# First three weight tiles side by side, and the operands of the first Strassen job, its silus and the last transposes made at other places, in a one-core encoder layer

## The chip, the cores and the metric

The kernel runs on one core of one Trainium2 chip. The metric is device time in microseconds (us) of one execution, lower is better. A profiled execution also leaves a trace: the rows of every engine (PE is the matrix engine, DVE, ACT and POOL the vector, scalar and GpSimd engines, SP the engine that issues most transfers) with start, length, and what ended the idle time before them.

## The reference

One layer of a streaming encoder on x of 512 tokens x 1024 channels, float32. Only what the change touches is shown.

```python
f = swiglu(rms_norm(h, ffn1_pre_g), w1, w3, w2)      # (silu(x @ w1) * (x @ w3)) @ w2, D_FF = 2816
h = h + 0.5 * rms_norm(f, ffn1_post_g)
u = rms_norm(h, mix_pre_g)
q, k, v, xr, xg = jnp.split(u @ w_in, splits, axis=-1)
...                                                  # recurrent branch, attention with a relative bias, gates
h = h + rms_norm(merged @ w_o, mix_post_g)
f = swiglu(rms_norm(h, ffn2_pre_g), v1, v3, v2)
h = h + 0.5 * rms_norm(f, ffn2_post_g)
```

## The kernel before

**Precision by splitting.** Every float32 operand of a product is split in two parts that PE takes at full rate: `hi` is a rounded copy made by ACT, `lo` the rest, made by DVE (`split2`, L182 to L185; `split_to`, L142 to L152 for weights). A product is three matmuls, hi x hi, lo x hi and hi x lo (L194 to L196 for 512 or 256 token columns in `mm_feat`; L212 to L214 in `mm_tok`; L440 to L442 in `mm_s`, 256 columns). `uT` holds the current activation, transposed and split, for all channels.

**Units.** A unit is one 128-row tile of a weight matrix against all tokens: 8 slices of 128 channels x 3 matmuls. The weights come in the order of the list `order`. `get` keeps a few units ahead: `dma_to` issues a tile's load (512 KB, on SP), `split_to` splits it.

**Slots.** Nearly all tiles in on-chip memory are taken from one pool of 42 slots of 4 KB per partition; a new tile takes the slot that has been free longest, and its first writer, a transfer or an engine, waits until the last reader of the tile before it is done. The transfers on SP also share eight completion semaphores in turn, so a ninth waits for the first. Products go to 8 PSUM banks.

**Order by hand.** The order of instructions on each engine is the order of the program. `later(n, fn)` puts a piece of work n points ahead; `point()` is called twice in each unit and once in each Strassen product and emits what is due. `point(True)` emits all that is left.

**The start** (L558 to L612). Nine matmuls on zeros warm PE up. The constants `vec`, the first weight tile in two parts and the eight slices of x (transposed) are loaded on SP, then three more weight tiles and the token-major copy `h`. Slice by slice, ACT and DVE scale x with the first norm's gain and split it into uT (L594, L595). Then three units run one after another on them, without the norm's factor 1/rms. That factor is computed from `h` meanwhile (squares L600, `rstd_of`), turned into `dgs`, a diagonal matrix per 128 tokens, and broadcast over partitions by PE (L609) into `Rb`; `silu_mul` (L393 to L404) applies it afterwards. Behind L609 stands a small product for the table of relative biases (L641). DVE copies it (L643), and one transfer issued by POOL writes it, repeated for 128 rows, to `bias_scr` in device memory (L646). Attention reads that much later.

**Units, then Strassen.** Tiles 2 to 5 of w1 and w3 of the first FFN run as units (`swiglu_units`). Meanwhile `norm_x` makes x normalised in plain float32 (`xn`), `sums` (L660) four sums of its quarters, and some of these quarters are split into slots of their own (`to_slots`). The rest of w1 and w3 is computed by `Pairs`: two weight tiles and the tokens in two halves, in 2 x 2 blocks, make one job with seven products in place of eight (Strassen's scheme in Winograd's form). A job needs its operands, made by `prep(m, i)`: i = 0 makes four sums of blocks of the weights (S12 and S34, on POOL, L482 to L485), i = 1, 2, 3 split the first tile, S12 and S34, i = 4 the block a22. `run` (L498 to L554) goes through the jobs, w1 and w3 in turn, and prepares job n + 1 between the products of job n. ACT copies out the partial results q1 (L513), q5 (L515), u (L520) and v (L532). Two banks, `bu` and `bx`, collect several products, so the next product into one waits for the copy of the last. The seventh product, a22 x t4, comes after two products of the next job (`last`). For w1's jobs the result c goes through a silu on ACT: two thirds of it at the job's end (L535, L536), the rest in `last` (L548). For job 0 four operands are written into uT (`to_uT`, L703 to L706), which only works after the last unit has read it.

The second FFN does the same (NC2 = 4 units' tiles there), with most of its operands from uT itself.

**The down projections and the wo product** (`tok_gemm`, L305). Four token tiles are finished one after another; each is normed (`norms`), transposed by PE (L285) and split into uT (L294, L295); for the second FFN a plain float32 copy `xf` is kept as well (L302). For the last tile PE meanwhile runs the first half of the tokens (columns 0 to 255) of the next four units (L374 to L381), then the last transposes (L382), then the second halves.

Of the kernel before, what the change touches and what calls it, by code (L numbers as in the profile page):

```python
# [10 lines left out]
F32 = mybir.dt.float32  # L11
# [4 lines left out]
P = 128  # L16
# [35 lines left out]
def hybrid_layer(ctx: ExitStack, tc: tile.TileContext, a: dict, out: bass.AP):  # L52
# [80 lines left out]

    def dma_to(n):
        while st["dma"] < min(n, len(order)):
            nm, i = order[st["dma"]]
            r = slot([P, D], name=f"raw_{nm}{i}")
            sp.dma_start(out=r, in_=a[nm][i * P : (i + 1) * P, :])
            raws[st["dma"]] = r
            st["dma"] += 1  # L140
# [76 lines left out]
    def rstd_of(ssq, scale=1.0, during=lambda: None):  # L217
# [9 lines left out]
        during()  # L227
# [17 lines left out]
    def post_norm(acc, t, gpost, scale, dst, after=None):  # L245
# [8 lines left out]
        r = rstd_of(ss, scale, lambda: dve.tensor_tensor(out=fg[:, cs[1]], in0=acc[1], in1=gpost[:, cs[1]], op=ALU.mult))  # L254
# [50 lines left out]
    def tok_gemm(nm, xs, n, R, gpost_name, scale, gpre_name, first, x_to=None, xf=None, spill=False):  # L305
# [139 lines left out]
    class Pairs:  # L445
# [3 lines left out]
        def __init__(self, na, nb, f0, X, hid):  # L449
# [3 lines left out]
            self.w, self.c1 = {}, {}  # L453
# [5 lines left out]
        def prep(self, m, i):  # L459
            if m >= len(self.jobs):  # L460
                return
            k = self.k0 + 2 * m
            if i == 0:
                self.raws(m)
# [16 lines left out]
            if i == 0:  # L481
                pool.tensor_tensor(out=s12[:, :QH], in0=a21, in1=a22, op=ALU.add)  # L482
                pool.tensor_tensor(out=s12[:, QH:], in0=s12[:, :QH], in1=a11, op=ALU.subtract)
                pool.tensor_tensor(out=s34[:, QH:], in0=a12, in1=s12[:, QH:], op=ALU.subtract)
                pool.tensor_tensor(out=s34[:, :QH], in0=a11, in1=a21, op=ALU.subtract)  # L485
# [12 lines left out]
        def run(self, tail):  # L498
# [4 lines left out]
            for n, (nm, f) in enumerate(self.jobs):  # L503
# [7 lines left out]
                bu, bx, bc = (bank("c")[:, :256] for _ in range(3))  # L511
                mm_s(W["a11"], X["b11"], bu)
                act.activation(q1, bu, AF.Copy)  # L513
# [20 lines left out]
                if first:  # L534
                    act.activation(c[:, 0, :], c[:, 0, :], AF.Silu)  # L535
                    act.activation(c[:, 1, 256:], c[:, 1, 256:], AF.Silu)  # L536
                else:
# [20 lines left out]
    raw = slot([P, D], name="raw_first")  # L558
    hi, lo = slot([P, D], F32R, name="whi"), slot([P, D], F32R, name="wlo")
    pairs[0] = (hi, lo)  # L560
    st["dma"] = st["split"] = 1
    parts = (slice(0, 2 * P), slice(2 * P, D))
    xts = [slot([P, 2, SEQ], name="xt") for _ in range(KT // 2)]

    def load_x(k):
        sp.dma_start(out=xts[k // 2][:, k % 2, :], in_=a["xT"][k * P : (k + 1) * P, :])
# [580 lines left out]
```

## Time and profile before

| | us |
|---|---|
| three runs | 1150.8, 1151.95, 1152.6 |
| median | 1151.95 |
| profiled execution | 1152.42 |
| its span, first to last instruction | 1150.6 |
| PE busy in it | 1133.9 |
| DVE, ACT, POOL busy | 781.1, 571.7, 355.3 |

The profile lists for each engine rows of the form: start, length (both us), engine, line, operation, output<-inputs, shapes, and in brackets how long the engine was idle before it and which instruction ended that. Matmuls overlap, so their lengths are longer than the distance between their starts; the pace of PE is read from the starts. "xN" at the end of a row means N equal instructions merged. A line such as L185 can be that of a helper: which tile it works on stands in the names.

### The profile page before, as it was taken

Reading aid. Unit: us, or ns where it says so; the run is one execution under the profiler, and the core shown is the slowest. Engines: PE = TensorE matmul, PEld = TensorE weight load, DVE = VectorE, ACT = ScalarE, POOL = GpSimd, SP = SyncE. Lnnn points to the kernel's source line nnn. Section 1 sums busy time; section 2 is a strip of 40 time slices with the busy share of each in tenths; the row PEclk is TensorE's granted clock in tenths of the full one; section 3 lists DMA queues with packets and bytes.
Section 4 is the critical chain, followed back from the end, with each engine's and each line's share of the span. In section 5 each row is a group of like instructions: output and inputs, shape, how many; then the busy total and the mean of one; then the engine's idle time right before and its main releaser. Section 6 shows DMA issues by size and latency. Waiting matters only on the chain.

```text
span 1150.6 us, 17044 instructions
## 1 busy us (share of the span) xinstructions
PE 1133.9 (99%) x6691; PEld 1008.4 (88%) x6691; DVE 781.1 (68%) x1168; ACT 571.7 (50%) x1011; POOL 355.3 (31%) x263
## 2 busy tenths in 40 slices
PE   8989999999999999999999999999999999999997
PEld 6879999988888888888888888889899999998886
DVE  4897788876427755595678864667868688885313
ACT  6345555564324457754656653355545555564211
POOL 0247777600001000001456550000655667700000
PEclk9999999999999999999999999999999999999999
DMA  9663332264312411234132223442033322255101
GB/s 361 108 131 100 111 111 92 76 218 157 105 68 94 164 55 56 73 110 144 41 92 92 79 89 126 149 144 92 19 111 111 106 88 101 93 183 170 50 19 55
DMA packets 35648, 124.93 MB, mean 109 GB/s; under 512 B 4272, under 2 KB 4400, under 8 KB 35568
## 3 DMA queue, kind: packets, MB, share of 16 engines
q1 hardware_dynamic: 33120, 115.41, 30.0%
q0 software_dynamic: 2448, 8.43, 3.9%
q8 instruction: 52, 0.85, 0.3%
q14 instruction: 28, 0.23, 0.1%
HBM read 116.50 MB, written 7.33 MB: 108 GB/s over the span
## 4 chain that ended last, share of the span: by engine, by line
PE 92%; DMA 3%; DVE 2%; ACT 1%; issue 1%; SPq 0%; DVEq 0%; ACTq 0%
PE f L196 11%; PE f L195 11%; PE f L194 11%; PE c L440 10%; PE c L442 10%; PE c L441 10%; PE acc L212 8%; PE acc L214 8%; PE acc L213 8%; DMA bias_scr<-erow 3%; PE pt L962 1%; PE s L926 1%; PE s L925 1%; PE o L978 1%; DMA raw_w3a<-in_w3a_dram 1%; PE o L979 1%
## 5 line engine op out<-in xcount | busy, mean ns | idle before, releaser
L194 PE MATMUL f<-uT,whi 128*128 128x512 f32 (+1 forms) x560 | 206.2, 368 | 2.2 <-ACT uT L594 1.7
L196 PE MATMUL f<-uT,whi 128*128 128x512 f32 (+1 forms) x560 | 205.2, 366 | 0.6 <-DVE uT L295 0.4
L195 PE MATMUL f<-uT,wlo 128*128 128x512 f32 (+1 forms) x560 | 204.8, 366 | 0.8 <-DVE wlo L150 0.8
L212 PE MATMUL acc<-whi,hT 128*128 128x512 f32 x352 | 137.3, 390 | 0.0
L213 PE MATMUL acc<-wlo,hT 128*128 128x512 f32 x352 | 137.1, 390 | 0.0
L214 PE MATMUL acc<-whi,hT 128*128 128x512 f32 x352 | 137.1, 389 | 0.0
L194 PEld LDWEIGHTS f<-uT,whi 128*128 128x128 f32 x560 | 105.7, 189 | 20.8 <-ACT uT L594 2.4
L196 PEld LDWEIGHTS f<-uT,whi 128*128 128x128 f32 x560 | 105.7, 189 | 19.1 <-DVE uT L595 1.3
L195 PEld LDWEIGHTS f<-uT,wlo 128*128 128x128 f32 x560 | 105.7, 189 | 17.6 <-DVE wlo L150 1.1
L185 DVE TENSOR_TENSOR wlo<-S,whi 128x1024 fp32r<-128x1024 f32 x68 | 115.0, 1691 | 8.8 <-ACT whi L184 6.9
L440 PE MATMUL c<-Xh,whi 128*128 128x256 f32 x408 | 116.3, 285 | 4.0 <-ACT ct L513 4.0
L441 PE MATMUL c<-Xh,wlo 128*128 128x256 f32 x408 | 116.2, 285 | 0.0
L442 PE MATMUL c<-Xl,whi 128*128 128x256 f32 x408 | 116.2, 285 | 0.0
L440 PE MATMUL c<-uT,whi 128*128 128x256 f32 x408 | 115.9, 284 | 0.0
L441 PE MATMUL c<-uT,wlo 128*128 128x256 f32 x408 | 115.8, 284 | 0.0
L442 PE MATMUL c<-uT,whi 128*128 128x256 f32 x408 | 115.8, 284 | 0.0
L440 PEld LDWEIGHTS c<-Xh,whi 128*128 128x128 f32 x408 | 78.8, 193 | 4.4 <-ACT ct L513 4.4
L946 POOL TENSOR_SCALAR P<-P,d 128x256 f32<-128x256 f32 (+1 forms) x64 | 63.0, 999 | 55.3 <-DVE d L944 33.6
L442 PEld LDWEIGHTS c<-Xl,whi 128*128 128x128 f32 x408 | 79.0, 194 | 0.0
L441 PEld LDWEIGHTS c<-Xh,wlo 128*128 128x128 f32 x408 | 78.9, 193 | 0.0
L440 PEld LDWEIGHTS c<-uT,whi 128*128 128x128 f32 x408 | 78.7, 193 | 0.0
L441 PEld LDWEIGHTS c<-uT,wlo 128*128 128x128 f32 x408 | 78.7, 193 | 0.0
(300 smaller groups left out, 2641.3 us busy)
## 6 DMA issues: line engine op xcount, KB each, us to landing
raw_w3a<-in_w3a_dram SPq DMA_DIRECT2D x22, 512.0 KB, 4.5
raw_w2a<-in_w2a_dram SPq DMA_DIRECT2D x22, 512.0 KB, 4.2
raw_w1b<-in_w1b_dram SPq DMA_DIRECT2D x22, 512.0 KB, 4.3
raw_w3b<-in_w3b_dram SPq DMA_DIRECT2D x22, 512.0 KB, 4.2
raw_w2b<-in_w2b_dram SPq DMA_DIRECT2D x22, 512.0 KB, 4.3
raw_w1a<-in_w1a_dram SPq DMA_DIRECT2D x21, 512.0 KB, 4.1
raw_wg<-in_wg_dram SPq DMA_DIRECT2D x16, 512.0 KB, 4.0
raw_xr<-in_xr_dram SPq DMA_DIRECT2D x8, 512.0 KB, 4.6
```

What stands on the lines that cost most here:

```text
L185: dve.tensor_tensor(out=lo, in0=src, in1=f32(hi), op=ALU.subtract)
L194: pe.matmul(ps[:, c0:c1], wh[:, s], h_, start=k == 0, stop=False)
L195: pe.matmul(ps[:, c0:c1], wl[:, s], h_, start=False, stop=False)
L196: pe.matmul(ps[:, c0:c1], wh[:, s], l_, start=False, stop=k == KT - 1)
L212: pe.matmul(acc[n], x[:, 0, c], wh[:, s], start=first, stop=False)
L213: pe.matmul(acc[n], x[:, 0, c], wl[:, s], start=False, stop=False)
L214: pe.matmul(acc[n], x[:, 1, c], wh[:, s], start=False, stop=last)
L440: pe.matmul(ps, wh[:, s], xh, start=first, stop=False, skip_group_check=True)
L441: pe.matmul(ps, wl[:, s], xh, start=False, stop=False, skip_group_check=True)
L442: pe.matmul(ps, wh[:, s], xl, start=False, stop=k == 3, skip_group_check=True)
L925: pe.matmul(o, lq, KS[g][:, 0, k0 : k0 + n], start=True, stop=False)
L946: pool.tensor_scalar(out=pt[:, x, b0:256], in0=pt[:, x, b0:256], scalar1=d[:, x : x + 1], scalar2=None, op0=ALU.mult)
```

## The change

- **Start.** Three weight tiles (w1 tile 0, w3 tile 0, w1 tile 1) are loaded in quarters between the slices of x, split in quarters, and for each slice of x PE runs nine matmuls, three for each tile. The first slice of x is issued by ACT, after a tiny square root there, which loads ACT's table. A tiny silu behind the square root of the norm loads the silu table early.
- **Bias table.** Its small product stands ahead of the broadcast of r, the copy is done by ACT, and the store is issued from there on.
- **Job 0 of the first FFN.** Its two weight tiles are loaded out of turn behind `h`. Its sums are made by DVE (behind `dgs`), its splits follow around the first `silu_mul`. Job 1's sums, first and second split are made before the jobs begin, at the places where job 0's stood before.
- **uT for job 0.** One of the four operands is written before job 0; the other three are emitted inside it, behind the copies of q1, q5 and u (`hooks`).
- **Silus.** All three of a w1 job are emitted in `last`, behind a22's product of the next job.
- **Last job of each FFN.** The a12 product stands behind s4 and s3 in place of ahead of them.
- **Last transposes.** They stand ahead of the fourth half unit, with the `xf` copies of the last two tiles behind them.

```diff
+    def dma_one(k):                      # loads order[k] out of turn
+        ...
     def dma_to(n):
         while st["dma"] < min(n, len(order)):
-            ...
+            dma_one(st["dma"])
             st["dma"] += 1
@@ rstd_of
         act.activation(q, v, AF.Sqrt)
-        during()
+        during(q)
@@ tok_gemm
         for i, key in enumerate(first):
             ws.append(get(*key, ahead=len(first) - 1 - i, rawahead=2))
             bs.append(bank("f"))
+            if i == len(first) - 1:
+                trs[t] = transpose_mm(us[t])
+                transpose_out(trs[t], t)
+                if xf:
+                    transpose_xf(trs[t - 1], t - 1, xf)
+                    transpose_xf(trs[t], t, xf)
             mm_feat(bs[i], ws[i], 0, 256)
             if i == 0:
-                tr = transpose_mm(us[t - 1])
+                trs[t - 1] = transpose_mm(us[t - 1])
                 us[t] = norms(acc[t], t, gpost, scale, gpre, spill)
-                transpose_out(tr, t - 1, xf)
-        transpose_out(transpose_mm(us[t]), t, xf)
+                transpose_out(trs[t - 1], t - 1)
@@ Pairs.prep
-        def prep(self, m, i):
-            if m >= len(self.jobs):
+        def prep(self, m, i, eng=None):
+            if m >= len(self.jobs) or (m, i) in self.ready:
                 return
...
-                pool.tensor_tensor(out=s12[:, :QH], in0=a21, in1=a22, op=ALU.add)
+                e = eng or pool
+                e.tensor_tensor(out=s12[:, :QH], in0=a21, in1=a22, op=ALU.add)
...
@@ Pairs.run
+                at = lambda i: [f() for f in hooks.get((n, i), ())]
                 mm_s(W["a11"], X["b11"], bu)
                 act.activation(q1, bu, AF.Copy)
+                at(1)
                 mm_s(W["s1"], X["t1"], bx)
                 act.activation(q5, bx, AF.Copy)
+                at(2)
                 last()
                 ...
                 act.activation(u, bu, AF.Copy)
+                at(3)
...
-                mm_s(W["a12"], X["b21"], bc)
-                del W["a11"], W["a12"]
-                dve.tensor_tensor(out=c[:, 0, :256], in0=bc, in1=q1, op=ALU.add)
+                def c11():
+                    mm_s(W["a12"], X["b21"], bc)
+                    del W["a11"], W["a12"]
+                    dve.tensor_tensor(out=c[:, 0, :256], in0=bc, in1=q1, op=ALU.add)
+                if n < len(self.jobs) - 1:
+                    c11()
...
                 dve.tensor_tensor(out=c[:, 1, 256:], in0=v, in1=q5, op=ALU.add)
-                if first:
-                    act.activation(c[:, 0, :], c[:, 0, :], AF.Silu)
-                    act.activation(c[:, 1, 256:], c[:, 1, 256:], AF.Silu)
-                else:
+                if n == len(self.jobs) - 1:
+                    c11()
+                if not first:
...
                     if first:
                         act.activation(c[:, 1, :256], bu, AF.Silu)
+                        act.activation(c[:, 0, :], c[:, 0, :], AF.Silu)
+                        act.activation(c[:, 1, 256:], c[:, 1, 256:], AF.Silu)
@@ start
+    tiny = small(4, "tiny")
+    dve.memset(tiny, 1.0)
+    act.activation(tiny, tiny, AF.Sqrt)
+    load_x(0, act)
     sp.dma_start(out=vec, in_=a["vec"])
-    sp.dma_start(out=raw[:, parts[0]], in_=a["w1a"][0:P, parts[0]])
-    load_x(0)
-    load_x(1)
-    sp.dma_start(out=raw[:, parts[1]], in_=a["w1a"][0:P, parts[1]])
-    for k in range(2, KT):
-        load_x(k)
-    dma_to(4)
+    for kp in range(KT // 2):
+        load_w(0, kp)
+        if kp:
+            load_x(2 * kp)
+        load_w(1, kp)
+        load_w(2, kp)
+        load_x(2 * kp + 1)
+    dma_to(NS + 2)
     h_load([a["x"][t * P : (t + 1) * P, :] for t in range(NT)])
+    pairs_a = Pairs("w1a", "w3a", NC1, X1, hid)
+    dma_one(pairs_a.k0)
+    dma_one(pairs_a.k0 + 1)
...
     for k in range(KT):
-        if k in (0, 2):
-            ...
+        if k % 2 == 0:
+            split_first(0, k // 2)
         act.activation(uT[:, 0, k, :], xk, AF.Copy, scale=g)
         dve.scalar_tensor_tensor(out=uT[:, 1, k, :], ...)
-    ps = [unit("w1a", 0), unit("w3a", 0), unit("w1a", 1)]
+        if k % 2 == 0:
+            split_first(1, k // 2)
+            split_first(2, k // 2)
+        s_ = slice(k * P, (k + 1) * P)
+        for (hi, lo), p_ in zip(pair3, ps):
+            pe.matmul(p_, hi[:, s_], uT[:, 0, k, :], start=k == 0, stop=False)
+            pe.matmul(p_, lo[:, s_], uT[:, 0, k, :], start=False, stop=False)
+            pe.matmul(p_, hi[:, s_], uT[:, 1, k, :], start=False, stop=k == KT - 1)
+    split_to(NS + 2)
...
-    r = rstd_of(s4)
+    r = rstd_of(s4, during=lambda q: act.activation(tiny, q, AF.Silu))
...
+    pairs_a.prep(0, 0, dve)
     ps.append(unit("w3a", 1))
+    pse = bank("e")                      # bias table: product, copy by ACT, store by POOL
+    ...
     for t in range(NT):
         pe.matmul(psr[:, t * P : (t + 1) * P], ones, dgs[:, t, :], start=True, stop=True)
     act.activation(Rb, psr, AF.Copy)
-    hid.f = [silu_mul(ps[0], ps[1], Rb), silu_mul(ps[2], ps[3], Rb)]
+    pairs_a.prep(0, 1)
+    hid.f += [silu_mul(ps[0], ps[1], Rb), silu_mul(ps[2], ps[3], Rb)]
+    pairs_a.prep(0, 2)
+    later(1, lambda: pairs_a.prep(0, 3))
+    later(2, lambda: pairs_a.prep(0, 4))
...
-    for i, at_ in enumerate((end - 8, end - 5, end - 4, end - 3, end - 2)):
-        later(at_, lambda i=i: pairs_a.prep(0, i))
-    later(end - 1, lambda: pairs_a.prep(1, 0))
+    for i, at_ in enumerate((end - 5, end - 2, end - 1)):
+        later(at_, lambda i=i: pairs_a.prep(1, i))
     swiglu_units("w1a", "w3a", 2, NC1, hid, Rb)
     point(True)
     X1["b21"] = to_uT(xn[1, 0], 1, 0)
-    X1["b22"] = to_uT(xn[1, 1], 1, 1)
-    X1["t3"] = to_uT(tn[2], 0, 1)
-    X1["t4"] = to_uT(tn[3], 0, 0)
+    late = {
+        (0, 1): [lambda: X1.update(b22=to_uT(xn[1, 1], 1, 1))],
+        (0, 2): [lambda: X1.update(t3=to_uT(tn[2], 0, 1))],
+        (0, 3): [lambda: X1.update(t4=to_uT(tn[3], 0, 0)), tn.clear, xn.clear],
+    }
...
-    pairs_a.run(w2_ahead)
+    pairs_a.run(w2_ahead, late)
```

More of the change, by code (lines that the diff above doesn't have):

```diff
@@ L496, in prep, with run @@
                 del W["r"], W["s"]
-        def run(self, tail):
+        def run(self, tail, hooks={}):
             X = self.X
@@ L554, in run, with load_x, load_w @@
             last()
[L558 to L562, printed above, removed]
-    xts = [slot([P, 2, SEQ], name="xt") for _ in range(KT // 2)]
-    def load_x(k):
-        sp.dma_start(out=xts[k // 2][:, k % 2, :], in_=a["xT"][k * P : (k + 1) * P, :])
+    NS = 3
+    raw3 = [slot([P, D], name="raw_first") for _ in range(NS)]
+    pair3 = [(slot([P, D], F32R, name="whi"), slot([P, D], F32R, name="wlo")) for _ in range(NS)]
+    st["dma"] = st["split"] = st["get"] = NS
+    xts = [slot([P, 2, SEQ], name="xt") for _ in range(KT // 2)]
+    def load_x(k, q=sp):
+        q.dma_start(out=xts[k // 2][:, k % 2, :], in_=a["xT"][k * P : (k + 1) * P, :])
+    def load_w(u, kp):
+        nm, i = order[u]
+        c = slice(kp * 2 * P, (kp + 1) * 2 * P)
+        sp.dma_start(out=raw3[u][:, c], in_=a[nm][i * P : (i + 1) * P, c])
     warm = slot([P, 512], F32R, name="warm")
@@ L677, in to_uT @@
         return uview(hh, th)
[L680 removed]
+    xn, tn = {(hh, th): slot([P, 4, 256], name="xn") for hh in range(2) for th in range(2)}, []
     def norm_x(k):
```

62 lines of the change are left out of this document (32 added, 30 removed).

## The prediction

> **What bounds the kernel now.** I read the page's busy times first, then TensorE's waits, then TensorE's rows in order of time at each wait, and last ACT, DVE, POOL and the transfers around them.
>
> ```profile
> span 1150.6 us, 17044 instructions
> ...
> PE 1133.9 (99%) x6691; PEld 1008.4 (88%) x6691; DVE 781.1 (68%) x1168; ACT 571.7 (50%) x1011; POOL 355.3 (31%) x263
> ```
> ```profile
> PE c L440 <- ACT ct L513: 4.0, 2, 3.1
> PE f L194 <- ACT uT L594: 1.7, 2, 1.3
> ...
> PE f L195 <- DVE wlo L150: 0.8, 1, 0.8
> PE c L440 <- ACT ct L532: 0.9, 2, 0.5
> ```
>
> TensorE (PE) is the bound: no other engine is near it, and the change takes no product from it. So the change can only win back time in which PE stands still or runs slowly. The second list (engine, line, who released it: total us, times, longest) has 7.4 us in these four rows, each at a place that the diff touches. Busy time hides what a slow matmul costs, so I measure from start to start.
>
> ```profile
> 75.81 0.39 PE L196 MATMUL f<-uT,whi 128*128 128x512 f32 x1
> ...
> 76.72 0.28 PE L440 MATMUL c<-Xh,whi 128*128 128x256 f32 x1
> ...
> 79.47 0.28 PE L442 MATMUL c<-Xl,whi 128*128 128x256 f32 x1
> 82.86 0.46 PE L440 MATMUL c<-Xh,whi 128*128 128x256 f32 x1 [3.11 <-ACT ct L513]
> ...
> 86.51 0.28 PE L442 MATMUL c<-uT,whi 128*128 128x256 f32 x1
> ```
>
> From 75.81 to 76.72 four products of 512 columns start: 0.2275 us each, the steady pace. From 76.72 to 79.47 it is 23 products of 256 columns, 0.12 us each. A unit (24 products of 512) is 5.46 us, one Strassen product (12 of 256) 1.44 us. After the stop, 17 starts from 82.86 to 86.51 take 3.65 us in place of 2.04: the pause of 3.1 us also costs 1.6 us of slow products behind it.
>
> **The start.** Before, the three first units ran one behind the other on what had landed; after, each k-slice of x is used for three weight tiles at once, nine products or 2.05 us for each slice.
>
> ```profile
> 5.51 0.50 PE L194 MATMUL f<-uT,whi 128*128 128x512 f32 x1 [0.31 <-ACT uT L594]
> ...
> 8.99 0.50 PE L194 MATMUL f<-uT,whi 128*128 128x512 f32 x1 [1.34 <-ACT uT L594]
> ...
> 31.34 1.05 PE L609 MATMUL r<-dgs,ones 128*128 128x128 f32 x8
> ...
> 33.06 0.50 PE L194 MATMUL f<-uT,whi 128*128 128x512 f32 x1
> ```
> ```profile
> 0.73 1.28 ACT L590 ACT_TABLE_LOAD   x1 [0.73 <-PEq L1135]
> ...
> 5.49 1.61 DVE L595 SCALAR_TENSOR_TENSOR uT<-xt,vec,uT 128x512 fp32r<-128x512 f32 x2 [1.14 <-ACT uT L594]
> ```
> ```profile
> DMA to landing us min/median/max: 3.0/5.4/5.8
> ```
>
> Four units are 96 products, 21.84 us; they took 31.34 - 5.51 = 25.83. So 4.0 us are lost there. After, the first slice of x is issued by ACT, behind the table load (0.73 + 1.28 = 2.0) and one tiny activation. With the shortest landing of x (3.0, third fence) it is there at about 5.2, against an issue at 1.64 and a first product at 5.51 before. I take the first product at 6.2; bounds 5.5 (the issue does not wait for the table) and 7.0. In the first slice the third product waits for DVE's part of x (0.8 of the 1.61 for two) behind two products (0.45): 0.3 us lost. From then on DVE needs 1.6 us for two slices and, for their three weight pieces, three quarter splits of at most 0.5 (the full one is 1.23, quoted below), 3.1 in all, ACT no more, PE 4.1: nothing is late. The fourth unit ends at 6.2 + 0.3 + 21.84 = 28.3. Gain 3.0 us (2.2 to 3.7). The broadcast of r and the small product for the bias table, 33.06 - 31.34 = 1.7 together, only change places, so the next unit starts at 30.0. The sums that go to DVE stand behind dgs there and don't hold the broadcast. The Silu table load leaves ACT's chain behind Rb, where PE had two units of cover: nothing.
>
> ```profile
> 2.00:3.00 1.00, 1.00 (x4) 0.77 (x3) 0.00 (x0) 0.01 (x1) 0.71 (x2) 1.00 0.94 167
> ...
> 10.00:12.00 2.00, 2.00 (x10) 1.55 (x10) 2.00 (x4) 2.00 (x4) 0.00 (x0) 1.00 1.06 425
> ```
>
> The last figure is GB/s. The twelve 128 KB pieces of weights and eight 256 KB slices of x, 3.7 MB from 2 us on, are there by 11 us at 425, by 24 at 167. The last pair of slices is wanted at 6.5 + 6 x 2.05 = 18.8, so 220 GB/s are enough; I take the small transfers as covered, nearer to the 425 of a filled queue. The Trainium skill, "DMA: Bandwidth & Descriptors", section "Measured (HBM→SBUF, 128 partitions, SWDGE, issued from GpSimd)", speaks against this edit: batch transfers to at least 1 MiB, smaller ones fall well below peak. What that would make of the time is the third rival.
>
> **Between start and first job.** The S sums of job 0 go from POOL to DVE and job 0's splits come at once: 4 sums, three wide splits and one half more on DVE ahead of the tail of norm_x.
>
> ```profile
> 32.43 0.60 ACT L610 ACTIVATE Rb<-r 128x512 f32<-128x512 f32 x1 [3.30 <-PE r L609]
> ```
> ```profile
> 54.56 2.31 DVE L150 TENSOR_TENSOR wlo<-raw_w3a,whi 128x1024 fp32r<-128x1024 f32 x1
> ...
> 72.19 1.23 DVE L185 TENSOR_TENSOR wlo<-S,whi 128x1024 fp32r<-128x1024 f32 x1 [1.68 <-DMA bias_scr<-erow]
> ```
>
> From Rb's end (33.03) DVE works almost without pause to 56.87, 23.8 us, the end of the split for w3a's tile 4, which PE wants at 33.06 + 5 x 5.46 + 0.2 = 60.6. The sums run before Rb and are free. After Rb come three splits of 1.23 and a half one of 0.6 (4.3), and 1.0 for the first of them to wait on ACT's part. What goes: about 1.2 for the copy of the bias table and the stop at the Silu table load (estimated from a load's 1.28), and POOL's disturbance, 1.1: the split at 54.56 took 2.31 while POOL summed, 1.23 at 72.19 without. 23.8 + 4.3 + 1.0 - 1.2 - 1.1 = 26.8 from Rb's end, now 30.6: 57.4, and PE wants it at 30.0 + 5 x 5.46 + 0.2 = 57.5. The cover is just used up: I charge 0.3 us (0 to 1).
>
> **The first job.** Before, four copies into uT stood on ACT ahead of the first evacuation, and the second product into that bank waits for it.
>
> ```profile
> 38.44 33.66 DMA bias_scr<-erow
> ...
> 78.67 3.88 ACT uT L184 x4
> ```
> ```profile
> 53.53 2.27 POOL L482 TENSOR_TENSOR S<-raw_w1a 128x512 f32<-128x512 f32 x1 [3.09 <-DMA raw_w1a<-in_w1a_dram]
> ...
> 73.89 1.30 POOL L482 TENSOR_TENSOR S<-raw_w3a 128x512 f32<-128x512 f32 x1 [11.40 <-DMA raw_w3a<-in_w3a_dram]
> ```
> ```profile
> DMA to landing us min/median/max: 7.9/14.4/20.9
> ```
>
> After, one copy (0.97) stands there, the others between the products of job 0. Counted from the end of PE's last unit, with 0.3 for an evacuation (82.86 less the end of the four copies, 82.55): copy 1.0, first evacuation 1.8, wanted at 2.9; then b22 at 2.8 and t3 at 4.2, with DVE's parts up to 2.3 each behind, wanted at 5.8 and 7.2. So the stop (82.86 - 79.59 = 3.3) and its slow products (1.6) go: 4.9. But next job's split of S12 now stands ahead of the silu and the copy on ACT, and its POOL sums wait for w3a's tile 7, whose slot comes free with the last product of w1a's tile 4. The trace (last fence: w3a's transfers from 38 us on) shows landings of 8 to 21 us while the 33.66 us store of the bias rows runs. That store now starts about 30 and ends about 64; the tile, issued at 30.0 + 5 x 5.46 = 57.3, lands at about 65.5. Two sums on POOL (1.3 to 2.3 each) give 68 to 70; the split, ACT's part and DVE's, 2.2 to 3.3; the product with Rb and the silu 0.7 each, an estimate from half a split; copy and evacuation 1.3: 73 to 76. PE reaches the end of its units at 30.0 + 8 x 5.46 = 73.7 and wants the evacuation at 76.6. DVE's own queue there, disturbed by POOL, adds about a microsecond. I charge 0.6 (0 to 2): gain 4.3 (2.9 to 4.9).
>
> **Silus, last jobs, last transposes.**
>
> ```profile
> 241.29 0.28 PE L442 MATMUL c<-uT,whi 128*128 128x256 f32 x1
> 242.05 0.39 PE L440 MATMUL c<-uT,w 128*128 128x256 f32 x1 [0.47 <-ACT ct L532]
> ...
> 377.44 1.04 PE L285 MATMUL tr<-ident,hg 128*128 128x128 f32 x8
> 378.73 0.38 PE L194 MATMUL f<-uT,whi 128*128 128x256 f32 x1 [0.25 <-ACT uT L294]
> ...
> 379.45 0.39 PE L196 MATMUL f<-uT,whi 128*128 128x256 f32 x1 [0.22 <-DVE uT L295]
> ...
> 805.48 1.04 PE L285 MATMUL tr<-ident,hg 128*128 128x128 f32 x8
> ...
> 853.49 0.28 PE L442 MATMUL c<-uT,w 128*128 128x256 f32 x1
> 854.64 0.39 PE L440 MATMUL c<-Xh,whi 128*128 128x256 f32 x1 [0.88 <-ACT ct L513]
> ```
> ```profile
> 371.79 0.72 ACT L276 ACTIVATE hg<-hg,r 128x512 f32<-128x512 f32 x1 [0.87 <-DVE r L236]
> ...
> 802.21 0.72 ACT L276 ACTIVATE hg<-hg,r 128x512 f32<-128x512 f32 x1 [0.87 <-DVE r L236]
> ...
> 853.38 0.42 ACT L536 ACTIVATE cc<-cc 128x256 f32<-128x256 f32 x1 [2.59 <-DVE cc L533]
> ```
>
> Silus: the first evacuation of pair job 1 in the second FFN stood behind a silu that waited 2.59 us for DVE. Moved behind the next job's a22 product, they wait where PE has two products (2.9 us) of cover before u is wanted: 854.64 - 853.61 = 1.0 gained. Last jobs: v's evacuation now has the a12 product (1.44) in front of a22: 242.05 - 241.41 = 0.64, and the same at the second (same row of the waits, two times): 1.3. The u evacuation loses one product of cover but keeps 1.44 against 0.4. Transposes: after them the next products lost 0.4 + 0.4. They now stand ahead of the fourth half unit (2.88), which covers their evacuation. In the first place the rows are ready at 372.5, before 377.44 - 2.88 = 374.6: 0.8 gained. In the second they are ready at 802.93, PE is there at 802.60: a new wait of 0.4, 0.4 gained. Moving the xf copies behind them adds to ACT only in front of splits due 11 us later.
>
> **Sum.** 3.0 - 0.3 + 4.3 + 1.0 + 1.3 + 1.2 = 10.5 us off the profiled execution's 1152.42 (1.8 more than its span), which lies 0.47 above the median of the runs: 1141.4. All bounds good (3.7, 0, 4.9, 1.0, 1.3, 1.6): 12.5 us, 1139.5; all bad (2.2, -1.0, 2.9, 1.0, 1.3, 1.2): 7.6, 1144.4.
>
> **Rivals.** (1) The first job's stop stays: POOL's S12 late, PE stops 3 us again and runs slowly behind. For it: landings of up to 21 us under the store; against: only two tiles are then in flight and the store ends ahead of them. The first job gives nothing: 1152.42 - 6.2 - 0.47 = 1145.8; 0.12. (2) A slow start: the ACT issue is late, the first product comes at 8.3, 3.1 us behind the warm-up, and the stop costs 1.6 of slow products as at 82.86: the start comes out 2.1 + 1.6 = 3.7 worse, 1145.1; 0.08. After the 1.34 us stop at 8.99 the pace was the steady one, so the point lies between. The Trainium skill, "TensorE: Matmul & The Clock Gate", section "Part 1: The HAM clock gate (the "warmup" mystery)", puts the idle window at about 3.4 us; the 3.11 us stop cooled the array here, so the trace's bound is lower; by the page's figure alone the slow products would not go with the stop and the sum would be 1.6 smaller. (3) Small transfers starve PE: at 167 GB/s throughout, 3.7 MB last to 24 us, 5.2 after the last slices are wanted: 1146.6; 0.04. This is what the batching rule of the Trainium skill's page above would come to. (4) Slower: the bias store, now started into a full weight queue, lasts longer. Each microsecond holds w3a's tile, POOL, ACT and job 0 by one; from 9 us longer (43) the gains are gone; at 50 us PE stops 17 us and the time is about 1159; 0.05. (5) The start, the first job and the transposes give nothing, each stop only moving on: 10.5 - 3.0 - 4.3 - 1.2 = 2.0 us left, 1149.9; 0.04. The forecast keeps 0.67.
>
> **Numbers.** 1141.4; the range 1139.0 to 1146.0 takes in the bounds, (1) and (2), and leaves (3) to (5) out. Within 0.2% (2.3 us) is what a measurement of this kernel can't tell from no change. Faster 0.91 (forecast and 1 to 3), same 0.04, slower 0.05.
>
> **What would show it.** Right: first product near 6.2, the r broadcast's first product near 29, no row of L440 waiting on the evacuation at 75 to 80, no wait before the last a22 and behind the transposes, one short wait before the second transposes. Wrong: PE rows with 0.21 us between 256-column products, PE waiting on wlo near 57, POOL's first sums after 71, a bias store of over 40 us.

## The result, and the profile after

The changed kernel takes 1140.29 us (median of 5 runs, 1140.08 to 1140.47), the kernel before 1152.6 (5 runs, 1150.8 to 1153.58): a ratio of 0.9895, 95% interval 0.9881 to 0.991. The profiled executions, 1152.42 and 1140.29 us, differ by 12.1.

The page of the changed kernel (span; busy time of each engine) and its list of what PE waited for (engine, line, releaser: total us, times, longest):

```profile
span 1138.5 us, 17073 instructions
...
PE 1129.9 (99%) x6691; PEld 1006.8 (88%) x6691; DVE 778.5 (68%) x1180; ACT 572.0 (50%) x1021; POOL 341.8 (30%) x259
```
```profile
PE w L602 <- DVE tiny L606: 1.4, 1, 1.4
PE f L201 <- DVE wlo L156: 0.3, 1, 0.3
```

The list has no further row. Of the four shown of before none is left; the first row is only the warm-up waiting for its zeros, the second is the new wait near 57 us. PE is still the bound, with the same 6691 products.

Where the time came from is read best from landmarks. PE's products are the same in both kernels, so away from the places where their order was changed the n-th from the end is the same product, and the difference of its starts is what has been won by then. PE rows in order of time, first of before, then of after (columns: start, us, engine, line, operands):

```profile
73.09 0.39 PE L196 MATMUL f<-uT,whi 128*128 128x512 f32 x1
...
103.66 0.28 PE L441 MATMUL c<-uT,w 128*128 128x256 f32 x1
...
252.67 0.39 PE L213 MATMUL acc<-wlo,hT 128*128 128x512 f32 x1
...
456.14 0.39 PE L194 MATMUL f<-uT,whi 128*128 128x512 f32 x1
...
845.45 0.28 PE L441 MATMUL c<-uT,wlo 128*128 128x256 f32 x1
...
906.57 0.28 PE L440 MATMUL c<-uT,whi 128*128 128x256 f32 x1
...
1143.42 0.39 PE L214 MATMUL acc<-whi,hT 128*128 128x512 f32 x1
```
```profile
70.16 0.39 PE L202 MATMUL f<-uT,whi 128*128 128x512 f32 x1
...
95.86 0.28 PE L452 MATMUL c<-uT,w 128*128 128x256 f32 x1
...
244.16 0.39 PE L219 MATMUL acc<-wlo,hT 128*128 128x512 f32 x1
...
446.61 0.39 PE L200 MATMUL f<-uT,whi 128*128 128x512 f32 x1
...
835.17 0.28 PE L452 MATMUL c<-uT,wlo 128*128 128x256 f32 x1
...
895.17 0.28 PE L451 MATMUL c<-uT,whi 128*128 128x256 f32 x1
...
1131.29 0.39 PE L220 MATMUL acc<-whi,hT 128*128 128x512 f32 x1
```

| stretch, ended by | start before | after | won in it | predicted |
|---|---|---|---|---|
| start: first product of the fifth unit | 33.06 | 29.59 | 3.5 | 3.0 |
| to the end of the units: wlo of w3a's tile 4 | 73.09 | 70.16 | -0.5 | -0.3 |
| first Strassen job | 103.66 | 95.86 | 4.9 | 4.3 |
| last job of the first FFN | 252.67 | 244.16 | 0.7 | 0.65 |
| first transposes | 456.14 | 446.61 | 1.0 | 0.8 |
| second transposes | 845.45 | 835.17 | 0.75 | 0.4 |
| pair job 1 of the second FFN (silus) | 906.57 | 895.17 | 1.1 | 1.0 |
| last job of the second FFN | 1143.42 | 1131.29 | 0.7 | 0.65 |
| sum | | | 12.1 | 10.5 |

Each landmark compares one execution of each kernel. Eight kernels of the experiments have the same first four units as the changed one, and in their traces the fifth unit begins at 29.32 to 30.09 us; so the start's 3.5 is good to about half a microsecond, though its rows are read to hundredths.

The start of the changed kernel, PE, then ACT with its queue:

```profile
5.57 0.80 PE L649 MATMUL f<-uT,whi 128*128 128x512 f32 x1
...
27.61 0.39 PE L202 MATMUL f<-uT,whi 128*128 128x512 f32 x1
...
29.59 0.48 PE L200 MATMUL f<-uT,whi 128*128 128x512 f32 x1
```
```profile
0.73 1.28 ACT L607 ACT_TABLE_LOAD   x1 [0.73 <-PEq L1192]
1.46 0.38 ACTq L590 DMA_DIRECT2D xt<-in_xT_dram  x1
...
4.79 0.72 ACT L642 ACTIVATE uT<-xt,vec 128x512 fp32r<-128x512 f32 x1 [0.81 <-DMA xt<-in_xT_dram]
```

From 5.57 to 27.61 stand 96 products without a recorded wait. ACT's queue issued the transfer at 1.46, in the middle of the table load; the prediction had it wait for the load's end.

Between start and first job, and the first job itself (PE, DVE, POOL, ACT and PE again, each its own view of the changed kernel):

```profile
57.56 0.50 PE L201 MATMUL f<-uT,wlo 128*128 128x512 f32 x1 [0.27 <-DVE wlo L156]
```
```profile
55.15 1.23 DVE L724 TENSOR_TENSOR T<-xn,T 128x1024 f32<-128x1024 f32 x1
56.29 1.22 DVE L156 TENSOR_TENSOR wlo<-raw_w3a,whi 128x1024 fp32r<-128x1024 f32 x1
```
```profile
65.74 1.29 POOL L496 TENSOR_TENSOR S<-raw_w3a 128x512 f32<-128x512 f32 x1 [13.57 <-DMA raw_w3a<-in_w3a_dram]
```
```profile
74.59 1.04 ACT L190 ACTIVATE uT<-xn 128x1024 fp32r<-128x1024 f32 x1
75.54 0.37 ACT L528 ACTIVATE ct<-c 128x256 f32<-128x256 f32 x1
```
```profile
76.66 0.28 PE L451 MATMUL c<-Xh,whi 128*128 128x256 f32 x1
```

The split of w3a's tile 4 ends at 57.51; PE's product starts 0.05 later, 0.66 behind the one before it (56.90, steady pace 0.23). In the first job the first evacuation (ACT's copy of a finished bank) ends at 75.91 and the product into the same bank starts at 76.66 on time: 0.75 us to spare.

### The profile page after: what moved, and what is told of

Read it like the earlier page. It is cut to its first block, busy times and chain, and to the rows that moved or that the text cites. A ratio compares the mean times of both kernels' runs of the same rounds, so it can differ in the third digit from the quotient of the medians.

```text
span 1138.5 us, 17073 instructions
## 1 busy us (share of the span) xinstructions
PE 1129.9 (99%) x6691; PEld 1006.8 (88%) x6691; DVE 778.5 (68%) x1180; ACT 572.0 (50%) x1021; POOL 341.8 (30%) x259
## 4 chain that ended last, share of the span: by engine, by line
PE 94%; DMA 4%; DVE 1%; SPq 0%; ACT 0%; issue 0%; DVEq 0%; ACTq 0%
PE f L201 11%; PE f L202 11%; PE f L200 11%; PE c L453 10%; PE c L452 10%; PE c L451 10%; PE acc L219 8%; PE acc L218 8%; PE acc L220 8%; DMA raw_w1a<-in_w1a_dram 2%; PE pt L1019 1%; DMA h<-in_x_dram 1%; PE s L983 1%; PE s L982 1%; PE tr L291 1%; PE o L1035 1%
## 5 line engine op out<-in xcount | busy, mean ns | idle before, releaser
L200 PE MATMUL f<-uT,whi 128*128 128x512 f32 (+1 forms) x536 | 196.1, 366 | 0.0
L201 PE MATMUL f<-uT,wlo 128*128 128x512 f32 (+1 forms) x536 | 195.2, 364 | 0.3 <-DVE wlo L156 0.3
L202 PE MATMUL f<-uT,whi 128*128 128x512 f32 (+1 forms) x536 | 195.1, 364 | 0.0
L201 PEld LDWEIGHTS f<-uT,wlo 128*128 128x128 f32 x536 | 101.2, 189 | 16.4 <-DVE wlo L156 0.7
L202 PEld LDWEIGHTS f<-uT,whi 128*128 128x128 f32 x536 | 101.1, 189 | 15.9
L200 PEld LDWEIGHTS f<-uT,whi 128*128 128x128 f32 x536 | 101.2, 189 | 15.6
L451 PEld LDWEIGHTS c<-uT,whi 128*128 128x128 f32 x408 | 78.3, 192 | 0.0
L453 PEld LDWEIGHTS c<-uT,whi 128*128 128x128 f32 x408 | 78.3, 192 | 0.0
```

Of the source, the lines that this page charges most:

```text
L200: pe.matmul(ps[:, c0:c1], wh[:, s], h_, start=k == 0, stop=False)
L201: pe.matmul(ps[:, c0:c1], wl[:, s], h_, start=False, stop=False)
L202: pe.matmul(ps[:, c0:c1], wh[:, s], l_, start=False, stop=k == KT - 1)
L451: pe.matmul(ps, wh[:, s], xh, start=first, stop=False, skip_group_check=True)
L453: pe.matmul(ps, wh[:, s], xl, start=False, stop=k == 3, skip_group_check=True)
```

## The experiments

Each kernel is the changed one with the edit shown, unless said otherwise; times are medians of the runs, "+" is against 1140.29. The kernel before ran beside them at 1152.2 to 1152.9.

**The start as before** (order of transfers and products; the rest of the start stays):

```diff
-    load_x(0, act)
     sp.dma_start(out=vec, in_=a["vec"])
-    for kp in range(KT // 2): ...            # weight pieces and slices of x in turn
+    load_w(0, 0); load_x(0); load_x(1); ...  # as before: the first tile, x, the other two tiles
...
+    for (hi, lo), p_ in zip(pair3, ps):      # the three units one after another
+        for k in range(KT): ...
```

> The changed kernel with only its start put back: vec, the first weight tile in two parts and x all on SP, the next two weight tiles whole behind x, and the first three units one after the other. Everything else stays as changed. Theory (the parts add, each as a stop of PE): the first product stays near 5.5, but the stops at the second slice pair and at the second unit come back, the broadcast of r starts about 31.3 as before, and the time rises by about 3.5 us (3.0 to 4.0) to about 1143.8. Rival (the early start only moves a later wait, so that the first job waits longer for the bias store and the tiles behind it): without it nothing is lost later either, and the time rises by less than 2 us.

1143.83 us (1143.6 to 1143.97), ratio to before 0.9927 (0.9912 to 0.9942): +3.5. PE waits again for the second slice of x (1.27 us at 9.04) and for a wlo (0.73 at 15.04), and the fifth unit begins at 33.01 in place of 29.59. So the start's whole gain is the order of products and transfers, the issue by ACT among them.

**The late copies made early again:**

```diff
-    late = {(0, 1): [lambda: X1.update(b22=...)], (0, 2): [... t3 ...], (0, 3): [... t4 ...]}
+    X1["b22"] = to_uT(xn[1, 1], 1, 1); X1["t3"] = to_uT(tn[2], 0, 1); X1["t4"] = to_uT(tn[3], 0, 0)
+    late = {}
```

> The changed kernel with the four operands in uT written ahead of job 0 again; the operands of jobs 0 and 1 are still made early. Theory (the copies ahead of the first evacuation are the stop): four copies from about 74.6 to 78.5, first evacuation at 78.5 to 78.8, wanted at 76.0, so PE stops 2.9 us and runs slowly behind it, in all +4.5 us (4.0 to 5.0), 1144.8. Rival (the operands of job 0 made early are what took the stop away, by relieving DVE): +1 us at most, 1141.3.

1143.07 us, but spread over 1141.7 to 1144.14 (0.992; 0.9905 to 0.9935): +2.8, less than the theory's 4.5. PE in the profiled execution, which took 1144.14:

```profile
78.87 0.39 PE L451 MATMUL c<-Xh,whi 128*128 128x256 f32 x1 [1.96 <-ACT ct L528]
...
82.49 0.41 PE L451 MATMUL c<-uT,whi 128*128 128x256 f32 x1
```

The stop is 2.0 us here, not 3.1 as in the kernel before: the early operands already shorten it. The theory had the evacuation right (it ends at 78.82), but PE wants the bank at 76.8 and not at 76.0. From 78.87 to 82.49 it is 18 starts, 3.6 us in place of 2.2. The granted clock (the mean share of PE's full clock that the profile records) is 0.996 in this execution and 0.999 in the one of 1141.7 us. So the slow products probably follow in some executions only. That is not shown: only one execution has a trace, and the one of 1141.7 us lies 1.4 above the changed kernel, less than this stop alone, so the stop was shorter there too, or time was won elsewhere.

**The same, with the stop filled** by 24 products of 256 columns into a spare bank (2.88 us of work whose result nobody reads):

```diff
+                if n == 0 and self.na == "w1a":
+                    for _ in range(2): mm_s(W["a11"], X["b11"], bd)
```

> e2's kernel with 24 extra products of 256 columns (2.9 us at full pace) into a spare bank in the place of the stop, so that PE isn't idle there; their result isn't used. Theory (the slow products behind the stop come from PE having been idle): the extra products fill the stop, those behind it run at 0.12 us, and the time is 1.6 us below e2's, near 1143.2. Rival (they are slow for another reason, such as operands read by PE while DVE writes them): the products behind stay at 0.21 us and the time is e2's.

1143.15 us (1142.97 to 1143.88): the changed kernel's time plus the 2.88 of the filling, to 0.02. With PE kept busy there are no slow products behind: from 79.33 on they start 0.12 us apart, although DVE writes uT beside them (78.03 to 81.48), so the rival is out. The executions lie closer together, but the median is no better than that of the open stop, of which I had expected 1144.8: the filling is longer than the stop.

**The first job's operands made at the old places** (the early calls of `prep` taken out, the old list of places put in):

```diff
-    pairs_a.prep(0, 0, dve) ... pairs_a.prep(0, 1) ... pairs_a.prep(0, 2) ... later(1, ...); later(2, ...)
-    for i, at_ in enumerate((end - 5, end - 2, end - 1)): later(at_, lambda i=i: pairs_a.prep(1, i))
+    for i, at_ in enumerate((end - 8, end - 5, end - 4, end - 3, end - 2)): later(at_, lambda i=i: pairs_a.prep(0, i))
+    later(end - 1, lambda: pairs_a.prep(1, 0))
```

> The changed kernel with the operands of job 0 made where they were before (sums on POOL, splits shortly before the jobs, its weight tiles loaded in turn), job 1's sums at the old place and its splits inside job 0; the copies into uT stay inside job 0. Theory (the copies' place is what counts, the early operands are second): no PE wait on wlo near 57, POOL disturbs DVE again from 50 on, DVE is late at the last unit, and the first evacuation comes up to 1.5 us late: +0.5 us (-0.4 to +2), 1140.8. Rival (the early operands carry the gain): the 3 us stop with its slow products comes back, +4 to +5, 1144.8.

1144.05 us (1142.62 to 1145.29; 0.9933, 0.9916 to 0.9949): +3.8. My theory of +0.5 fell; the rival was right that the early operands carry much of the gain, but not that the 3 us stop comes back as one: two shorter ones do. PE and DVE of the profiled execution, the quickest of the four:

```profile
77.15 0.39 PE L451 MATMUL c<-Xh,whi 128*128 128x256 f32 x1 [0.84 <-ACT ct L528]
...
86.19 0.39 PE L452 MATMUL c<-Xh,wlo 128*128 128x256 f32 x1 [1.46 <-DVE wlo L191]
```
```profile
81.58 2.32 DVE L191 TENSOR_TENSOR uT<-T,uT 128x1024 fp32r<-128x1024 f32 x1
83.83 2.30 DVE L191 TENSOR_TENSOR wlo<-S,whi 128x1024 fp32r<-128x1024 f32 x1
```

The second stop is new. The late copies have a DVE part each, and the next job's splits stand behind them; with POOL's sums running beside, two of these take 2.3 us in place of 1.2, and the split of S is 1.5 us late. Made early, the same operands leave DVE free for the copies: in the changed kernel the last two DVE parts stand at 78.22 and 79.66, with no split between them.

**The late copies alone, on the kernel before:**

```diff
+    late = {(0, 1): [... b22 ...], (0, 2): [... t3 ...], (0, 3): [... t4 ...]}   # nothing else changed
```

> The kernel before with one edit alone: three of job 0's four operands in uT are written inside job 0. Theory: the 3.1 us stop shrinks to the 0.4 us that DVE's lateness leaves (the copy starts at 78.7, the first evacuation at 79.7, wanted at 79.6), the slow products go with it: 4.3 us less than before (3.5 to 4.9), near 1148. Rival: without the early operands the stop stays near 3 us, since job 0's own splits now push the copies: less than 2 us.

1152.18 us (10 runs) against 1152.93: ratio 0.9998 (0.9989 to 1.0008), nothing gained. PE and DVE:

```profile
90.23 0.58 PE L441 MATMUL c<-Xh,wlo 128*128 128x256 f32 x1 [2.73 <-DVE wlo L185]
```
```profile
83.42 2.32 DVE L185 TENSOR_TENSOR wlo<-raw_w3a,whi 128x1024 fp32r<-128x1024 f32 x1
85.67 2.30 DVE L185 TENSOR_TENSOR uT<-T,uT 128x1024 fp32r<-128x1024 f32 x1
87.89 2.28 DVE L185 TENSOR_TENSOR wlo<-S,whi 128x1024 fp32r<-128x1024 f32 x1
```

The stop of 3.1 us at 83 is down to 0.26, and one of 2.73 stands 10 us later, in the next job. It only moved on, onto DVE: the second product of that job waits for the third of three splits at 2.3 us each.

**Both edits of the first job undone:**

> The changed kernel with both edits of the first job as before: all four copies into uT ahead of it, and its first operands made at the old places on POOL. Copies alone back cost 2.8 us, operands alone back 3.8, the late copies alone on the kernel before gained 0.0. Theory: the two edits only work together, since the copies moved between the products need a DVE that isn't also making the next job's splits; so with both back the loss is that of the stop of before, about 3.1 us and 1.6 of slow products, less 0.4 since the short wait for a wlo near 57 us goes: 1140.3 + 4.3 = 1144.6 us, far less than 2.8 + 3.8 more. Rival: the losses add, 1140.3 + 6.6 = 1146.9, with a second stop behind the one at 80.

1145.68 us (1145.03 to 1146.43; 0.9946, 0.9932 to 0.9961): +5.4, between the two. PE:

```profile
80.32 0.58 PE L451 MATMUL c<-Xh,whi 128*128 128x256 f32 x1 [3.65 <-ACT ct L528]
...
85.60 0.36 PE L451 MATMUL c<-uT,whi 128*128 128x256 f32 x1
```

One stop, as the theory had it, and no second one, but 0.5 longer than before's and the 24 starts from 80.32 to 85.60 take 5.3 us in place of 2.9 (17 slow ones before). Either edit alone keeps 1.6 to 2.6 of these 5.4 us on the changed kernel (medians of four runs that spread over up to 2.7 us). On the kernel before the late copies alone keep nothing, but there the bias store still stands at its old place: the tile for job 1's sums lands at 73.43, behind the store's end at 71.81, and the sums begin at 73.59 in place of 65.74. So the 4.9 of the first job belong to the pair of edits, not to one, and the early store, undone next, is a condition for both.

**The bias store later** (its copy and transfer three points on, about 11 us):

```diff
-    act.activation(erow, ...); pool.dma_start(out=scr, ...)
+    later(3, bias_out)
```

> The changed kernel with the copy and the store of the bias table three points (8 us) later, about where they stood before. Theory (the store holds w3a's tile 7, that holds POOL's sums of job 1, these hold ACT and DVE ahead of the first evacuation): the store ends at about 74, the tile lands at 75.5, S12 is there at 78.5, the first evacuation comes at 84 to 85 in place of 75.5, PE stops 8 to 9 us, with slow products behind: +9 us (7 to 11), 1149. Rival (the tile's landing hides behind other work, the early store is worth nothing): within 0.5 us of the changed kernel.

1150.04 us (10 runs; 0.998, 0.997 to 0.9989): +9.75, as the theory said. PE, then the list of transfers from 25 to 80 us (KB each, median us to landing), then the same list of the changed kernel from 25 to 70:

```profile
84.04 0.58 PE L451 MATMUL c<-Xh,whi 128*128 128x256 f32 x1 [7.24 <-ACT ct L528]
```
```profile
bias_scr<-erow POOLq DMA_DIRECT2D x1, 3064.0 KB, 33.4
raw_w3a<-in_w3a_dram SPq DMA_DIRECT2D x3, 512.0 KB, 18.3
raw_w1a<-in_w1a_dram SPq DMA_DIRECT2D x1, 512.0 KB, 5.4
```
```profile
bias_scr<-erow POOLq DMA_DIRECT2D x1, 3064.0 KB, 33.6
raw_w3a<-in_w3a_dram SPq DMA_DIRECT2D x3, 512.0 KB, 12.9
raw_w1a<-in_w1a_dram SPq DMA_DIRECT2D x1, 512.0 KB, 23.3
```

Issued at 40.86 the store lasts to 74 instead of 63 us, w3a's tile 7 lands at 75.31 instead of 65.58, POOL's sums start at 75.47 instead of 65.74, and the first evacuation, behind them on ACT, ends at 83.98, 8.1 later than in the changed kernel. Of these 0.75 were to spare: a stop of 7.2, and slow products behind it. The chain of tile, POOL, ACT and job 0 that the fourth rival priced is there. The loss of 9.75 is more than the 4.9 won in that job, so by this sum the pair of edits is worth nothing without the early store.

**The silus as before:**

```diff
+                if first: act.activation(c[:, 0, :], ..., AF.Silu); act.activation(c[:, 1, 256:], ..., AF.Silu)
-                        (the same two behind the a22 product)
```

> The changed kernel with two of the three silus of each w1 job at the job's end again. Theory: only the stop of the second FFN's pair job 1 comes back, 0.9 us of idle PE and 0.1 of refilling near 842 of the changed kernel's time: +1.0 us (0.8 to 1.2), 1141.3. Rival: in the first FFN job 0 to 1, where DVE is behind as well, a second such stop appears: +2 us.

1140.47 us (1140.33 to 1140.83): +0.2, not +1.0, and no wait of PE there. The 0.2 can't be told from nothing: in the trace of this run the fifth unit, ahead of anything the edit touches, already begins 0.40 us later than in the changed kernel (29.99).

**Last jobs and transposes as before:**

```diff
-                if n < len(self.jobs) - 1: c11()       # and c11() of the last job behind v
+                c11()
-            if i == len(first) - 1: ... transposes ahead of the last half unit
+        transpose_out(transpose_mm(us[t]), t, xf)      # behind it
```

> The changed kernel with the a12 product of each FFN's last job and the last transposes of both down projections at their old places. Theory: two waits of 0.47 (0.64 from start to start) before the last a22 and two pairs of 0.25 + 0.22 (0.8 from start to start) behind the transposes come back, less the 0.2 that PE now loses ahead of the second transposes: +2.7 us (2.4 to 3.0), 1143.0. Rival: the waits are covered now by other moves, below +1 us.

1143.82 us (1143.47 to 1144.0): +3.5, against 3.2 from the landmarks (two times 0.7, 1.0, 0.75); all six waits are back, none at the silus. In its trace the last product comes 3.7 later than in the changed kernel, 0.5 of it from the start, whose code is the same. The second FFN's stop stays away whichever of the two edits is undone, so both were undone together.

**Silus and transposes as before:**

> The changed kernel with the silus and the last transposes both as before (silus alone back cost 0.2 us). Theory: the two edits each remove the same stop of 1.0 us ahead of the second product of pair job 1 in the second FFN. Moving the transposes brings the load of the next tile, and with it POOL's sums, forward, so that they no longer run beside DVE's part of job 0; with both back POOL's first sums run beside it again (DVE splits of about 2.1 in place of 1.2), the silu waits over 2 us for DVE, and PE waits about 0.9 there: 1140.3 + 1.7 (transposes) + 1.1 = 1143.1 us. Rival: the silus' place is worth nothing in any case, the other gains having moved DVE's work away from it: no row of PE waiting there, 1140.3 + 1.7 + 0.2 = 1142.2.

1143.45 us (1142.25 to 1144.2). PE, ACT, DVE and POOL of it; then DVE and POOL of the run with the silus alone as before, whose times lie 2.26 us earlier:

```profile
847.13 0.39 PE L446 MATMUL c<-Xh,whi 128*128 128x256 f32 x1 [0.87 <-ACT ct L523]
```
```profile
845.87 0.42 ACT L556 ACTIVATE cc<-cc 128x256 f32<-128x256 f32 x1 [2.94 <-DVE cc L551]
```
```profile
842.19 2.21 DVE L191 TENSOR_TENSOR wlo<-S,whi 128x1024 fp32r<-128x1024 f32 x1
844.33 1.51 DVE L551 TENSOR_TENSOR cc<-ct 128x256 f32<-128x256 f32 x1
```
```profile
838.23 2.28 POOL L494 TENSOR_TENSOR S<-raw_w1b,raw_w1b 128x512 f32<-128x512 f32 x1
842.02 1.30 POOL L491 TENSOR_TENSOR S<-raw_w3b 128x512 f32<-128x512 f32 x1 [1.51 <-PE c L448]
```
```profile
838.62 1.22 DVE L191 TENSOR_TENSOR wlo<-S,whi 128x1024 fp32r<-128x1024 f32 x1
840.14 1.21 DVE L556 TENSOR_TENSOR cc<-ct 128x256 f32<-128x256 f32 x1 [0.30 <-ACT ct L555]
```
```profile
832.92 2.28 POOL L499 TENSOR_TENSOR S<-raw_w1b,raw_w1b 128x512 f32<-128x512 f32 x1
```

The stop is back with both undone, and with neither undone alone (in the profiled execution a second one, 0.71 at 87.66, stands at the same place of the first FFN). POOL's four sums ahead of it end at 840.51 here; with the transposes moved they end at 835.20, which is 837.46 on this clock, 3 us earlier. The splits behind them are then done sooner: the last one starts at 838.62 (840.88 on this clock) in place of 842.19, takes 1.22 and ends as POOL's next sums begin (839.76). Here the next sums begin at 842.02, the split of 842.19 runs beside them and takes 2.21, and the silu waits 2.94 for DVE in place of 0.76.

**A version made from this**: the first slice of x issued first on SP and `vec` by ACT, seven warm-up matmuls, and the `sums` call two points later:

```diff
-    load_x(0, act)
-    sp.dma_start(out=vec, in_=a["vec"])
+    act.dma_start(out=vec, in_=a["vec"])
+    load_x(0)
-    later(6, lambda: tn.extend(sums(xn)))
+    later(8, lambda: tn.extend(sums(xn)))
```

> The changed kernel with three small edits: SP issues the first slice of x as its first transfer and ACT issues the constants, so that the slice is there at about 4.0 in place of 4.7; seven warm-up matmuls in place of nine; and the sums of norm_x two points later on POOL, so that the split of w3a's tile 4 does not run beside them. Theory: the first product near 4.9 in place of 5.6, of which up to 0.3 is given back at the second slice of x; the wait of 0.3 us on wlo near 57 (0.43 from start to start) goes: 0.4 to 1.1 less, 1139.4 us. Rival: the constants land later through ACT and hold the first copy of x, and the sums, moved on, come late for the first products of pairs: no gain at the start, a new wait near 62 to 70, 1140.3 or more.

1139.84 us (1139.62 to 1140.02, all below the changed kernel's runs); 0.9896 of before (0.9879 to 0.9912): 0.45 less, within the theory's 0.4 to 1.1. The wait for the wlo is gone, 0.57 by the landmarks. It went for a reason other than the one I wrote: three of the four sums stand on DVE, right ahead of that split (the last at 55.15, above), and moved they stand behind it. The start gave only 0.09. The first product came at 4.99, but the other pieces came later (ACT; the first weight piece of w3a):

```profile
5.80 0.75 ACT L190 ACTIVATE whi<-raw_first 128x256 fp32r<-128x256 f32 x2 [0.86 <-DMA raw_first<-in_w3a_dram]
```

In the changed kernel the same two pieces are copied from 5.42 on, without a wait.

## Why the prediction was right, step by step

- **Sum**: 10.5 predicted, 12.1 in the trace, 1141.4 against 1140.29. All eight rows of the table have the predicted sign and come within 0.6 us; the sum is short since all but one are short on the same side. Undone group by group (start, pair of the first job, ends, silus), the edits cost 3.5 + 5.4 + 3.5 + 0.2 = 12.6 us, near the 12.3 between the medians.
- **Start** (3.0, measured 3.5): the step that failed is the queue behind the table load. The issue came at 1.46 and the first product at 5.57, the bound of 5.5, not 6.2. The 0.3 charged for DVE's part of the first slice came as 0.43 of slow starts without a recorded wait (the first three distances are 0.59, 0.27 and 0.27). The rest holds: the fourth unit ends at 27.61 + 0.23 = 27.84 against 28.3, and the first product behind the broadcast comes at 29.59 against 30.0.
- **Small transfers** (third rival): the 96 products run without a wait, so pieces of 128 KB kept up. The batching rule of the Trainium skill, "DMA: Bandwidth & Descriptors", section "Measured (HBM→SBUF, 128 partitions, SWDGE, issued from GpSimd)", did not decide here.
- **Between** (0.3, measured 0.5): "the cover is just used up" was right: the split ended at 57.51 by the trace, 57.4 by the working. Its price was 0.2 short; part of that is the product itself, 0.05 between the split's end and the start, and a slower first start behind a wait.
- **First job** (4.3, measured 4.9): the whole stop went, and the 0.6 charged for the late POOL sums was not needed. Their chain came as worked out: tile to land at 65.5, landed at 65.58, POOL at 65.74; evacuation done between 73 and 76, measured 75.91; wanted at 76.6, measured 76.66. What the prediction didn't see is that the two edits need each other, and both the early store (late copies alone on the kernel before: 0.0).
- **Silus** (1.0, measured 1.1 in its stretch): the time is there, but not by the reason given alone. Moving the transposes alone removes the same stop, and beside it the silus' new place is worth 0.2 at most. I took the 2.59 us wait for DVE as a fixture of the place; it came from POOL's sums beside DVE's splits.
- **Last jobs** (1.3, measured 1.4): as worked out. **Transposes** (1.2, measured 1.8): the new wait before the second ones, priced at 0.4, is 0.06 of standing still and 0.22 from start to start, so 0.75 is won there; in the first place the two waits of 0.4 were worth 1.0 with the slower starts behind them.
- **The rivals**: a stop in the first job (1) comes back with either edit alone, but held by the four copies or by DVE, not by POOL's late sums as (1) had it. The slow start (2) did not come, with the first product at 5.57. That a stop only moves on (5) is what the late copies alone do. The longer store (4) did not come: 33.6 us, 33.66 before, though started into a full queue; the loads beside it gave way. But with the store issued 11 us later all but 2 us of the gain are gone, so its mechanism was rightly named.

## What to carry to other kernels

A stop taken away by moving work on one engine can simply move to the engine that does the second half of that work: look whether that engine has room at the new place, and make room first. Two edits can hold the same stop away, so undoing one shows nothing; undo them in pairs before calling one useless. Landmarks counted from the end of a fixed sequence of products say where time was won in a pair of executions, to a few hundredths, where medians scatter by half a microsecond; what varies between executions, such as the pace of the first products and behind a stop, is in them too.

## What the runs showed of the hardware beyond that

- **Short stops and the clock.** Behind a stop of 1.96 us 18 starts took 3.6 us in place of 2.2 in one execution, while another execution of the same kernel was 2.4 us shorter at a granted clock of 0.999. Behind the stop of 2.73 us of the late copies alone 11 products start 0.21 apart. Behind stops of 1.46, 1.34 (kernel before, at 8.99) and 1.27 us the pace was the steady one after one to three slower starts. The Trainium skill, "TensorE: Matmul & The Clock Gate", section "Part 1: The HAM clock gate (the "warmup" mystery)", gives an idle window of about 3.4 us; here the slow pace followed a stop of 1.96 us in the one execution that has a trace. The kernel before, whose stop is 3.1 us, spreads over 2.8 us in its runs, the changed kernel, which has none, over 0.4; that the stop is the cause of the spread is likely, not shown.
- **The first products' pace.** The slow pace of the warm-up (0.43 between 512-column starts) ended between 4 and 7.6 us, differing between kernels whose start is the same: the run with the silus alone back had its first real products 0.43 apart up to 7.59 and was 0.4 us behind the changed kernel by the fourth unit (25.07 against 24.66), nearly all of its 0.5 us longer span. The same section says that the number of cold matmuls varies from run to run with the phase of the window; the traces agree that it varies; the phase is in none of them.
- **The store and the loads.** The store of 3064 KB issued by POOL takes 33.4 to 34.3 us in all 13 traces, whatever runs beside it. The 512 KB loads issued while it runs land 7.9 to 28.2 us after their issue in the traces of the kernel before and the changed one, against 3.7 to 4.7 us for those issued in the 20 us behind its end.
